# One encoder layer on one core: transposes and attention steps emitted at other places, row steps of two gate blocks reordered, finer splits, x loaded earlier

## The chip, the cores and the metric

The kernel runs on 1 core of one Trainium2 chip. The metric is the device time of one execution in microseconds. Before the change the median of 3 runs is 2099.92 us (2099.83 to 2100.81).

## What is computed

One layer of a bidirectional encoder for 256 tokens of width 2048, all in float32: a half-step SwiGLU feed-forward network (inner width 5632), a mixer of two attentions side by side, and a second half-step SwiGLU. Norms stand ahead of and behind each part.

```
def swiglu(h, w_gate, w_up, w_down):
    return (jax.nn.silu(h @ w_gate) * (h @ w_up)) @ w_down

f = swiglu(rmsnorm(x, ffn1_pre_g), ffn1_w_gate, ffn1_w_up, ffn1_w_down)
x = x + 0.5 * rmsnorm(f, ffn1_post_g)
h = rmsnorm(x, mix_pre_g)
qa, ka, va, qb, kb, vb, ga, gb = jnp.split(h @ w_in, SPLITS, axis=-1)
ga, gb = sigmoid(ga + bias_a), sigmoid(gb + bias_b)
out_a = windowed_gqa_sink(rope(qa), rope(ka), va, sink)              # 8 query heads, 2 key heads
out_b = differential_attention(rope(qb), rope(kb), vb, lam, subln_g) # 4 heads, two softmaxes each
x = x + rmsnorm((ga * (out_a @ w_proj_a) + gb * (out_b @ w_proj_b)) @ w_out, mix_post_g)
f = swiglu(rmsnorm(x, ffn2_pre_g), ffn2_w_gate, ffn2_w_up, ffn2_w_down)
x = x + 0.5 * rmsnorm(f, ffn2_post_g)
```

## The kernel before

The 256 tokens are two halves h0 and h1 of 128. A matrix product in float32 is three TensorE passes on parts rounded to a shorter format, hi and lo (`mm3`, `mm3s`: hi by hi, lo by hi, hi by lo; L257 to L259 in wide blocks, L200 to L202 elsewhere). All 400 MB of weights come from HBM in **units** of 1 MB (`load_unit`, on SP's queue). `emit_upto` splits each unit: ACT copies it to the short format (hi, the cast at L177), DVE subtracts to get lo (L179). A unit is one 128x2048 instruction on each, or four of 128x512 for unit 0 (L183). Two units are split ahead of the one in use.

A **tall** block makes 512 columns for both halves (`run_block`). A **wide** block makes 1024 columns for both halves in four banks (`run_wide`); its units are row steps of 256 rows, and each is N (24 matmuls, plain) or S (a Strassen step: seven products instead of eight, on sums of the weights that DVE makes at L188 to L190 and on sums of the inputs from `make_forms`, L394 to L402). `SKIND = "NSNSNSNN"` gives the kinds of the eight row steps of a gate or up block. Behind the last S step the extra products are folded into the banks: ACT copies one bank (L292), DVE adds the rest (L293 to L305). Only then do the banks come free for the block behind.

The blocks run in this order: ffn1; kb0, kb1, qb, vb, kv; ga0, qa, gb0, ga2 (gates and queries); the two branch projections and wo; ffn2. In each FFN column block 0 is tall; the first wide gate block, c == 1, is the one where the inputs' sums are made beside the matmuls.

What isn't on the main path is put between the matmuls. `later(fn, n)` defers a function by n calls of `pump()`, which each row step makes once. The rotary result of a query or key block (L641 to L648 on DVE) is transposed by TensorE in such a deferred function (`split_T`, L407, with the copies L408 on ACT and L409 on DVE), and so are the products of gate and up. The attentions are `pipeline`s of items: `ItemB` (8 items, stages s0 to s3 at L709 to L750) beside kv and ga0, `ItemA` (8 items, three stages, L766 to L807) beside gb0 and ga2; each `pump()` issues one step of the pipeline. `drain()` pumps until nothing is left, with no matmul between; it stands ahead of each pipeline and behind ga2. A gate block ends in four DVE instructions at L836 and four sigmoids on ACT at L839.

The order on each engine is not the order of the code: a scheduler of the compiler, with its own idea of the durations, places every instruction by its release and its priority. `tc.high_priority(HP)` lifts what it encloses. Each engine then runs its instructions strictly in that order and waits where one isn't ready.

Of the kernel before, what the change touches and what calls it, by code (L numbers as in the profile page):

```python
# [35 lines left out]
SKIND = "NSNSNSNN"  # L36
HP = 300
# [6 lines left out]
def encoder_layer(  # L44
# [89 lines left out]
    def add_wide(w, r0, rows, c0, kinds=None):  # L134
        kinds = kinds or "N" * (rows // 256)
        return add_units(w, r0, rows, c0, kinds), kinds

    loaded, emitted = {}, {}
    spill, paced = set(), set()
    lo_of, hi_of = {}, {}  # L140
# [25 lines left out]
    def emit_upto(i):  # L166
        for k in range(len(emitted), min(i + 1, len(units))):
# [58 lines left out]
    def run_block(start, nu, lhs, after, lag=0, pre=None, tail=None):  # L226

        acc = [acc_tile(), acc_tile()]
        for i in range(nu + lag):
# [12 lines left out]
            for h, u in ((0, i), (1, i - lag)):  # L242
# [8 lines left out]
                if u == nu - 1:  # L251
                    after(h, 0, acc[h])
# [8 lines left out]
    def run_wide(block, lhs, forms, after):  # L261


        start, kinds = block
        last_s = kinds.rfind("S")
        bank, opened = {}, set()
        end = len(kinds) - 1
# [8 lines left out]
        for u, kind in enumerate(kinds):  # L276
            w = weights(start + u)
            if kind == "S":
# [6 lines left out]
                order = ("P1", "P2", "P6", "Q5", "P3", "P7", "Q4") if u == last_s else                     ("P1", "P2", "P3", "Q5", "P7", "P6", "Q4")  # L285
                for o in order:
                    f = open_(o)
                    mm3s(bank[o], *ops[o], f, u == last_s, True)
                if u == last_s:
# [16 lines left out]
            else:  # L306
                order = (("P2", 0, 0), ("P3", 0, 1), ("X", 1, 1), ("Q4", 1, 0)) if last_s >= 0 else                     (("P2", 0, 0), ("P3", 0, 1), ("Q4", 1, 0), ("X", 1, 1))
                for o, h, c in order:
                    t = lhs(u, h)
                    for j in range(2):  # L310
                        f = open_(o)
                        closes = u == end or u == last_s - 1 and o == "X"
                        mm3s(bank[o], (t[:, 0, j, :], t[:, 1, j, :]), w, 2 * j + c, f, closes and j == 1, last_s >= 0)
                    if u == end:
# [154 lines left out]
    def ffn(post_g, pre, plan, lag, final, tail, x_src):  # L469
# [5 lines left out]
        def gate_up(c0, run_gate, run_up):  # L475
# [6 lines left out]
            def up_after(h, c, acc):  # L482
# [7 lines left out]
                later(tr, 2 if c0 + 1 in last_c or c0 == 0 else len(SKIND) - 1)  # L490
# [39 lines left out]
    def plan_ffn(w_gate, w_up, w_down):  # L530
        pl = {"gate": {}, "up": {}, "down": {}}
        for part, (c_lo, c_hi) in enumerate(PARTS):
            for c in range(c_lo, c_hi):
# [3 lines left out]
                elif c % 2:  # L537
                    pl["gate"][c] = add_wide(w_gate[0], 0, D, c * NC, SKIND)
# [28 lines left out]
    for b in (pm["kb", 0], plan2["gate"][0]):  # L567
        spill.add(b)
        paced.add(b + 3)

# [8 lines left out]
    load_unit(0, (2, 3))  # L579
    for h in range(2):  # L580
        load_x(h, 256, 1024)
    load_upto(1)
# [229 lines left out]
    def pipeline(items, offs):  # L812
        n = len(items)
        for t in range(n + offs[-1]):
# [10 lines left out]
    drain()  # L825
    ticker[0] = pipeline([ItemB(s, h, hh) for s in range(2) for h in range(2) for hh in range(2)], (0, 1, 2, 3))
# [38 lines left out]
    drain()  # L865
# [62 lines left out]
```

## Time and profile before

| what | value |
|---|---|
| median of 3 runs | 2099.92 us |
| the profiled execution | 2102.28 us |
| span of its trace, first to last instruction | 2100.5 us |
| TensorE (PE) busy | 2045.2 us, 97% |
| VectorE (DVE) busy | 1430.9 us, 68% |
| ScalarE (ACT) busy | 987.4 us, 47% |
| mean granted TensorE clock | 0.989 |
| DMA, mean over the span | 198 GB/s |

The page gives shares of the whole span. PE is nearly always busy, so what it loses lies in a few places, and those are found with the view of PE's waits and read in the timeline of the stretch: each row has the start, the length, the instruction, and in brackets the idle time before it and what ended it. A bracket of one engine names the instruction on another engine; that engine's timeline of the same stretch says why it came late.

### The profile page before, as it was taken

Reading aid. Unit: us, or ns where it says so; the run is one execution under the profiler, and the core shown is the slowest. Engines: PE = TensorE matmul, PEld = TensorE weight load, DVE = VectorE, ACT = ScalarE, POOL = GpSimd, SP = SyncE. Lnnn points to the kernel's source line nnn. Section 1 sums busy time; section 2 is a strip of 40 time slices with the busy share of each in tenths; the row PEclk is TensorE's granted clock in tenths of the full one; section 3 lists DMA queues with packets and bytes.
Section 4 is the critical chain, followed back from the end, with each engine's and each line's share of the span. In section 5 each row is a group of like instructions: output and inputs, shape, how many; then the busy total and the mean of one; then the engine's idle time right before and its main releaser. Section 6 shows DMA issues by size and latency. Waiting matters only on the chain. (4 is left out here: it accounts for less than half of the span.)

```text
span 2100.5 us, 22846 instructions
## 1 busy us (share of the span) xinstructions
PE 2045.2 (97%) x9193; PEld 1680.1 (80%) x9193; DVE 1430.9 (68%) x1400; ACT 987.4 (47%) x943; POOL 56.2 (3%) x91
## 2 busy tenths in 40 slices
PE   8999999999999989999899999999999999999997
PEld 6788887888877878888788888787888788887786
DVE  5884798647986575676664555577658885588854
ACT  6454455435553453455454344455454544454442
POOL 1000000000000010000000000000000000000000
PEclk9999999999999999999999999999999999999999
DMA  8546555676557646554445556554575565856662
GB/s 289 185 170 231 201 180 196 214 211 200 186 195 291 208 162 204 193 175 158 153 151 188 203 189 243 199 186 149 216 232 188 196 214 187 225 181 211 232 252 86
DMA packets 140571, 416.36 MB, mean 198 GB/s; under 512 B 8415, under 2 KB 9233, under 8 KB 139185
## 3 DMA queue, kind: packets, MB, share of 16 engines
q1 hardware_dynamic: 133872, 391.15, 54.0%
q0 software_dynamic: 6560, 23.75, 4.1%
q8 instruction: 72, 1.18, 0.2%
q14 instruction: 35, 0.28, 0.0%
q10 hardware_dynamic: 32, 0.01, 0.0%
HBM read 400.19 MB, written 14.68 MB: 198 GB/s over the span
## 5 line engine op out<-in xcount | busy, mean ns | idle before, releaser
L179 DVE TENSOR_TENSOR w<-raw,w 128x2048 fp32r<-128x2048 f32 (+2 forms) x365 | 796.5, 2184 | 500.3 <-ACT w L177 465.8
L177 ACT CAST w<-raw 128x2048 fp32r<-128x2048 f32 (+2 forms) x365 | 666.7, 1828 | 783.8 <-PE acc L258 605.4
L257 PE MATMUL acc<-w,xT 128*128 128x512 f32 x1368 | 536.6, 393 | 5.6 <-ACT t L292 4.0
L258 PE MATMUL acc<-w,xT 128*128 128x512 f32 x1368 | 534.1, 390 | 0.0
L259 PE MATMUL acc<-w,xT 128*128 128x512 f32 x1368 | 512.5, 391 | 0.6 <-DVE w L179 0.6
L257 PE MATMUL acc<-w,big 128*128 128x512 f32 x828 | 323.2, 391 | 3.3 <-ACT w L177 3.3
L258 PE MATMUL acc<-w,big 128*128 128x512 f32 x828 | 323.8, 391 | 0.0
L259 PE MATMUL acc<-w,big 128*128 128x512 f32 x828 | 317.6, 390 | 0.2 <-DVE w L179 0.2
L257 PEld LDWEIGHTS acc<-w,xT 128*128 128x128 f32 x1368 | 257.5, 188 | 61.9 <-ACT t L292 4.8
L259 PEld LDWEIGHTS acc<-w,xT 128*128 128x128 f32 x1368 | 257.5, 188 | 54.8 <-DVE w L179 1.4
L258 PEld LDWEIGHTS acc<-w,xT 128*128 128x128 f32 x1368 | 257.6, 188 | 52.0
L257 PEld LDWEIGHTS acc<-w,big 128*128 128x128 f32 x828 | 155.7, 188 | 36.4 <-ACT w L177 4.1
L259 PEld LDWEIGHTS acc<-w,big 128*128 128x128 f32 x828 | 155.6, 188 | 32.5 <-DVE w L179 0.6
L258 PEld LDWEIGHTS acc<-w,big 128*128 128x128 f32 x828 | 155.7, 188 | 31.9
L177 ACT CAST big<-raw 128x2048 fp32r<-128x2048 f32 x62 | 118.6, 1913 | 93.1 <-DVE raw L190 89.1
L179 DVE TENSOR_TENSOR big<-raw,big 128x2048 fp32r<-128x2048 f32 x62 | 141.2, 2286 | 20.7 <-ACT big L177 15.8
L201 PE MATMUL acc<-w,xT 128*128 128x512 f32 x208 | 83.0, 401 | 3.0 <-DVE xT L358 3.0
L200 PE MATMUL acc<-w,xT 128*128 128x512 f32 x208 | 82.0, 399 | 0.0
L202 PE MATMUL acc<-w,xT 128*128 128x512 f32 x208 | 80.4, 393 | 0.0
L257 PE MATMUL acc<-big,big 128*128 128x512 f32 x180 | 72.3, 402 | 6.1 <-ACT big L177 6.1
L200 PE MATMUL acc<-w,big 128*128 128x512 f32 x192 | 74.7, 389 | 0.0
L201 PE MATMUL acc<-w,big 128*128 128x512 f32 x192 | 74.7, 389 | 0.0
(186 smaller groups left out, 1744.7 us busy)
## 6 DMA issues: line engine op xcount, KB each, us to landing
raw<-in_ffn_w_down SPq DMA_DIRECT2D x88, 1024.0 KB, 5.2
raw<-in_w_in SPq DMA_DIRECT2D x68, 1024.0 KB, 5.0
raw<-in_ffn_w_up SPq DMA_DIRECT2D x58, 1024.0 KB, 5.1
raw<-in_ffn_w_gate SPq DMA_DIRECT2D x57, 1024.0 KB, 5.1
raw<-in_ffn_w_gate SPq DMA_DIRECT2D x60, 512.0 KB, 4.7
raw<-in_ffn_w_up SPq DMA_DIRECT2D x60, 512.0 KB, 4.7
raw<-in_w_out SPq DMA_DIRECT2D x16, 1024.0 KB, 5.0
f_dram<-t POOLq DMA_DIRECT2D x32, 256.0 KB, 5.8
```

The costliest lines, as they stand in the source:

```text
L177: nc.scalar.copy(hi[:, sl], raw[:, sl])
L179: nc.vector.tensor_tensor(lo[:, sl], raw[:, sl], f32(hi[:, sl]), ALU.subtract)
L200: nc.tensor.matmul(o, lhi, rhi, start=first, stop=False)
L201: nc.tensor.matmul(o, llo, rhi, start=False, stop=False)
L202: nc.tensor.matmul(o, lhi, rlo, start=False, stop=last)
L257: nc.tensor.matmul(o, t[0], w[0][:, q, :], start=first, stop=False, skip_group_check=skip)
L258: nc.tensor.matmul(o, t[1], w[0][:, q, :], start=False, stop=False, skip_group_check=skip)
L259: nc.tensor.matmul(o, t[0], w[1][:, q, :], start=False, stop=last, skip_group_check=skip)
```

## The change

The order of the row steps of the first wide gate block (c == 1) in both FFNs goes through a table, `FIRST`: N N S N S N S N instead of N S N S N S N N, with the same weights to the same inputs. Some units are split in two pieces of 1024 columns (`fine`): units 1 to 3, and five units each around the start of kb0 and of ffn2; unit 0 stays in four. `after` of a tall block is issued at high priority. The transposes of gate times up are deferred by 8 pumps instead of 7. At the start the columns 256 to 1024 of x are loaded ahead of the second half of unit 0, and the columns 1024 to 2048 ahead of unit 1. Both drains ahead of the attention pipelines and the one behind ga2 are gone: the pipelines wait 1 and 3 pumps first, in which the deferred transposes are issued beside matmuls. Lines of the changed kernel stand 1 to 5 further on (L407 becomes L409, L736 L740, L836 L841).

```diff
+FIRST = (0, 2, 1, 4, 3, 6, 5, 7)
...
-    def add_units(w, r0, rows, c0, kinds):
+    def add_units(w, r0, rows, c0, kinds, order=None):
 
         start = len(units)
-        r = r0
-        for k in kinds:
-            n, c = (512, NC) if k == "T" else (256, 2 * NC)
-            units.append((k, w[r:r + n, c0:c0 + c]))
-            r += n
-        assert r == r0 + rows
+        for i in order or range(len(kinds)):
+            n, c = (512, NC) if kinds[i] == "T" else (256, 2 * NC)
+            units.append((kinds[i], w[r0 + i * n:r0 + (i + 1) * n, c0:c0 + c]))
...
-                for j in [slice(i, i + 1) for i in range(4)] if k == 0 else [slice(0, 4)]:
+                for j in [slice(i, i + fine.get(k, 4)) for i in range(0, 4, fine.get(k, 4))]:
                     split(hi, lo, j)
...
                 if u == nu - 1:
-                    after(h, 0, acc[h])
+                    with tc.high_priority(HP):
+                        after(h, 0, acc[h])
...
-        for u, kind in enumerate(kinds):
-            w = weights(start + u)
+        for n, (u, kind) in enumerate(steps):
+            w = weights(start + n)
...
-                later(tr, 2 if c0 + 1 in last_c or c0 == 0 else len(SKIND) - 1)
+                later(tr, 2 if c0 + 1 in last_c or c0 == 0 else len(SKIND))
...
-                    pl["gate"][c] = add_wide(w_gate[0], 0, D, c * NC, SKIND)
+                    pl["gate"][c] = add_wide(w_gate[0], 0, D, c * NC, SKIND, FIRST if c == 1 else None)
...
+        fine.update({b + i: 2 for i in range(-1, 4)})
+
+    fine.update({0: 1, 1: 2, 2: 2, 3: 2})
...
     load_x(1, 0, 256)
-    load_unit(0, (2, 3))
     for h in range(2):
         load_x(h, 256, 1024)
-    load_upto(1)
+    load_unit(0, (2, 3))
     for h in range(2):
         load_x(h, 1024, 2048)
     load_upto(2)
...
-    def pipeline(items, offs):
+    def pipeline(items, offs, wait):
         n = len(items)
+        for _ in range(wait):
+            yield
...
-    drain()
-    ticker[0] = pipeline([ItemB(s, h, hh) for s in range(2) for h in range(2) for hh in range(2)], (0, 1, 2, 3))
+    ticker[0] = pipeline([ItemB(s, h, hh) for s in range(2) for h in range(2) for hh in range(2)], (0, 1, 2, 3), 1)
...
-    drain()
-    ticker[0] = pipeline([ItemA(h, p) for h in range(2) for p in range(4)], (0, 1, 2))
+    assert ticker[0] is None
+    ticker[0] = pipeline([ItemA(h, p) for h in range(2) for p in range(4)], (0, 1, 2), 3)
     gate_block("gb", D, 0)
     ga0, gb0 = gates.pop("ga"), gates.pop("gb")
     gate_block("ga", 0, 2)
-    drain()
+    assert ticker[0] is None
```

The diff doesn't tell where the instructions stand on their engines. First place, PE in the first wide gate block of ffn1, from the closing of the last Strassen bank to the first matmul of the up block (the first into `acc_917` before, into `acc_923` now); `big_` weights are the sums. Before:

```order
L259 MATMUL acc_676<-w_735,xT_295 128x512
L259 MATMUL acc_619<-w_735,xT_295 128x512
L259 MATMUL acc_626<-w_735,big_603 128x512
L257 MATMUL acc_917<-w_837,xT_134 128x512
L258 MATMUL acc_917<-w_837,xT_134 128x512
L257 MATMUL acc_694<-big_741,big_603 128x512
```

Now:

```order
L261 MATMUL acc_712<-w_771,xT_301 128x512
L261 MATMUL acc_625<-w_771,xT_301 128x512
L261 MATMUL acc_632<-w_771,big_601 128x512
L259 MATMUL acc_722<-big_708,big_582 128x512
L260 MATMUL acc_722<-big_708,big_582 128x512
L259 MATMUL acc_726<-big_708,big_582 128x512
L260 MATMUL acc_726<-big_708,big_582 128x512
L259 MATMUL acc_730<-big_708,big_582 128x512
L260 MATMUL acc_730<-big_708,big_582 128x512
L259 MATMUL acc_646<-big_708,xT_235 128x512
L260 MATMUL acc_646<-big_708,xT_235 128x512
L259 MATMUL acc_923<-w_834,xT_134 128x512
```

Before, two matmuls stand between the bank's last one (`acc_676`) and the up block's first; now ten stand there behind the last into `acc_712`. In all, PE's rows change only at the start, in these two blocks of each FFN, at the last matmuls ahead of kb0 and of ffn2, and from ga0 to ga2.

Second place, DVE at the end of ga0, where the last item of the B attention ends; `t_1083` before and `t_1086` now are its result (L736, L740), which PE transposes right ahead of qa; L325 and L327 make the norm's factor for it, and `w_` is the split of a unit. Before:

```order
L836 SCALAR_TENSOR_TENSOR t_1095_6841<-acc_6361,pnr_5259,t_991_6351 128x512
L836 SCALAR_TENSOR_TENSOR t_1097_6851<-acc_6368,pnr_5259,t_992_6353 128x512
L325 TENSOR_SCALAR bv_6780<-bss_6778 128x1
L836 SCALAR_TENSOR_TENSOR t_1098_6860<-acc_6375,pnr_5345,t_991_6351 128x512
L750 SCALAR_TENSOR_TENSOR big_6674<-tp_6785,gT,big_6674 128x128
L836 SCALAR_TENSOR_TENSOR t_1099_6869<-acc_6382,pnr_5345,t_992_6353 128x512
L736 TENSOR_SCALAR t_1083_6777<-at_6770,br_6782 128x256
L179 TENSOR_TENSOR w_6875<-raw_6872,w_6874 128x2048
```

Now:

```order
L841 SCALAR_TENSOR_TENSOR t_1094_6850<-acc_6328,pnr_5275,t_976_6318 128x512
L841 SCALAR_TENSOR_TENSOR t_1096_6860<-acc_6335,pnr_5275,t_977_6320 128x512
L841 SCALAR_TENSOR_TENSOR t_1097_6869<-acc_6342,pnr_5361,t_976_6318 128x512
L841 SCALAR_TENSOR_TENSOR t_1098_6878<-acc_6349,pnr_5361,t_977_6320 128x512
L180 TENSOR_TENSOR w_6891<-raw_6888,w_6890 128x2048
L327 TENSOR_SCALAR bv_6826<-bss_6824 128x1
L754 SCALAR_TENSOR_TENSOR big_6720<-tp_6831,gT,big_6720 128x128
L740 TENSOR_SCALAR t_1086_6823<-at_6816,br_6828 128x256
```

The result stood behind the fourth L836 and ahead of the unit's split; now its factor and it stand behind both the four L841 and the split.

Third place, PE from qa (bank `acc_1106`, short `acc_6899` and `acc_6915`) to gb0; `tp` is a transposed rotary result. Before:

```order
L259 MATMUL acc_6899<-w_7029,xT_5248 128x512
L407 MATMUL tp_7141<-ident,t_1128_7098 128x128 x4
L407 MATMUL tp_7149<-ident,t_1130_7110 128x128 x4
L407 MATMUL tp_7156<-ident,t_1132_7122 128x128 x4
L407 MATMUL tp_7163<-ident,t_1134_7134 128x128 x4
L257 MATMUL acc_7180<-w_7058,xT_5043 128x512
```

Now:

```order
L261 MATMUL acc_7187<-w_7075,xT_5055 128x512
L259 MATMUL acc_7166<-w_7104,xT_5082 128x512
L409 MATMUL tp_7195<-ident,t_1128_7114 128x128 x4
L260 MATMUL acc_7166<-w_7104,xT_5082 128x512
L261 MATMUL acc_7166<-w_7105,xT_5082 128x512
L259 MATMUL acc_7166<-w_7104,xT_5082 128x512
```

Before, the four transposes stood between the two blocks. Now the first stands behind 25 matmuls of gb0 (the rows above begin with the 24th), the second 12 further on, the third and the fourth together another 11 behind it.

## Rows read from the trace of the kernel before

**Rows 1.** Section 1 of the page: busy us, share of the span, instructions.
```profile
span 2100.5 us, 22846 instructions
...
PE 2045.2 (97%) x9193; PEld 1680.1 (80%) x9193; DVE 1430.9 (68%) x1400; ACT 987.4 (47%) x943; POOL 56.2 (3%) x91
```

**Rows 2.** Waits of PE: line waited for, us in total, times, longest.
```profile
PE tp L407 <- DVE t L648: 6.5, 3, 2.8
PE acc L257 <- ACT big L177: 6.1, 6, 1.5
```

**Rows 3.** Timeline of PE at the start: start us, us, instruction, [idle before <-releaser].
```profile
10.40 0.69 PE L350 MATMUL tp<-ident,big 128*128 128x128 f32 x2 [3.77 <-DMA big<-in_x]
...
11.72 0.78 PE L200 MATMUL acc<-w,xT 128*128 128x512 f32 x1
```

**Rows 4.** Timeline of ACT at the start.
```profile
14.05 1.91 ACT L177 CAST w<-raw 128x2048 fp32r<-128x2048 f32 x1 [1.32 <-DMA raw<-in_ffn_w_gate]
```

**Rows 5.** DMA view, 0 to 24 us: GB/s in 40 equal slices.
```profile
GB/s 0 0 5 189 177 360 331 352 312 111 52 195 335 399 410 422 405 410 396 393 403 389 430 416 382 396 389 386 393 389 382 382 389 386 386 389 386 393 386 382
```

**Rows 6.** Line L179 by form: xcount, duration ns min/median/max, forms.
```profile
L179 DVE TENSOR_TENSOR w<-raw,w x365: 691/2291/2294, 4.9 to 2076.3; 128x2048 fp32r<-128x2048 f32 x121, 128x1536 fp32r<-128x1536 f32 x60, 128x512 fp32r<-128x512 f32 x2
```

**Rows 7.** Timeline of PE, first wide gate block of ffn1.
```profile
91.87 0.50 PE L257 MATMUL acc<-w,xT 128*128 128x512 f32 x1 [2.19 <-ACT t L292]
...
93.75 0.79 PE L257 MATMUL acc<-big,big 128*128 128x512 f32 x1 [1.14 <-ACT big L177]
94.34 0.63 PE L258 MATMUL acc<-big,big 128*128 128x512 f32 x1
...
96.87 0.39 PE L258 MATMUL acc<-big,xT 128*128 128x512 f32 x1
```

**Rows 8.** Windows: us, busy (x) of PE, PEld, DVE, ACT, POOL, granted PE clock, DMA share, GB/s.
```profile
55.00:97.00 42.00, 38.37 (x164) 30.53 (x163) 39.50 (x47) 24.65 (x20) 0.00 (x0) 0.96 0.54 185
...
1012.00:1029.00 17.00, 10.52 (x45) 8.24 (x44) 14.53 (x22) 5.44 (x6) 0.00 (x0) 0.80 0.59 208
```

**Rows 9.** Timeline of PE, first wide gate block of ffn2.
```profile
1437.72 0.50 PE L257 MATMUL acc<-w,xT 128*128 128x512 f32 x1 [1.79 <-ACT t L292]
...
1440.00 0.79 PE L257 MATMUL acc<-big,big 128*128 128x512 f32 x1 [1.48 <-ACT big L177]
```

**Rows 10.** Timeline of PE, end of ffn1 to kb0.
```profile
746.18 1.11 PE L350 MATMUL tp<-ident,big 128*128 128x128 f32 x4 [3.73 <-DVE big L421]
```

**Rows 11.** Timeline of PE, end of ga0.
```profile
972.90 0.44 PE L746 MATMUL tp<-ident,t 128*128 128x128 f32 x2 [1.48 <-DVE t L736]
...
973.41 0.40 PE L258 MATMUL acc<-w,xT 128*128 128x512 f32 x1
973.64 0.40 PE L259 MATMUL acc<-w,xT 128*128 128x512 f32 x1
```

**Rows 12.** Timeline of DVE, end of ga0.
```profile
964.90 0.15 DVE L325 TENSOR_SCALAR bv<-bss 128x1 f32<-128x1 f32 x1 [0.45 <-ACT t L734]
...
965.78 0.48 DVE L736 TENSOR_SCALAR t<-at,br 128x256 f32<-128x256 f32 x1 [0.27 <-POOL br L327]
...
969.42 1.40 DVE L836 SCALAR_TENSOR_TENSOR t<-acc,pnr,t 128x512 f32<-128x512 f32 x2
...
970.80 0.74 DVE L836 SCALAR_TENSOR_TENSOR t<-acc,pnr,t 128x512 f32<-128x512 f32 x1
...
974.21 2.29 DVE L179 TENSOR_TENSOR w<-raw,w 128x2048 fp32r<-128x2048 f32 x1 [1.37 <-ACT w L177]
```

**Rows 13.** Timeline of PE, end of qa.
```profile
1018.01 0.66 PE L407 MATMUL tp<-ident,t 128*128 128x128 f32 x4 [1.10 <-DVE t L648]
1021.46 0.82 PE L407 MATMUL tp<-ident,t 128*128 128x128 f32 x4 [2.80 <-DVE t L648]
1024.86 1.97 PE L407 MATMUL tp<-ident,t 128*128 128x128 f32 x8 [2.58 <-DVE t L648]
```

**Rows 14.** Timeline of DVE, end of qa.
```profile
1024.13 1.29 DVE L648 TENSOR_TENSOR t<-t,t 128x512 f32<-128x512 f32 x2
```

More of the change, by code (lines that the diff above doesn't have):

```diff
@@ L118, in encoder_layer @@
     units = []
-    def add_units(w, r0, rows, c0, kinds):
+    def add_units(w, r0, rows, c0, kinds, order=None):
         start = len(units)
-        r = r0
-        for k in kinds:
-            n, c = (512, NC) if k == "T" else (256, 2 * NC)
-            units.append((k, w[r:r + n, c0:c0 + c]))
-            r += n
-        assert r == r0 + rows
+        for i in order or range(len(kinds)):
+            n, c = (512, NC) if kinds[i] == "T" else (256, 2 * NC)
+            units.append((kinds[i], w[r0 + i * n:r0 + (i + 1) * n, c0:c0 + c]))
+        assert n * len(kinds) == rows
         return start
@@ L132, in add_tall, with add_wide @@
         return add_units(w, r0, rows, c0, "T" * (rows // 512))
-    def add_wide(w, r0, rows, c0, kinds=None):
+    def add_wide(w, r0, rows, c0, kinds=None, order=None):
         kinds = kinds or "N" * (rows // 256)
-        return add_units(w, r0, rows, c0, kinds), kinds
+        order = order or range(len(kinds))
+        return add_units(w, r0, rows, c0, kinds, order), [(u, kinds[u]) for u in order]
     loaded, emitted = {}, {}
     spill, paced = set(), set()
+    fine = {}
     lo_of, hi_of = {}, {}
@@ L261, in run_wide @@
     def run_wide(block, lhs, forms, after):
-        start, kinds = block
-        last_s = kinds.rfind("S")
+        start, steps = block
+        last_s = max([n for n, (_, k) in enumerate(steps) if k == "S"], default=-1)
         bank, opened = {}, set()
-        end = len(kinds) - 1
+        end = len(steps) - 1
         def open_(o):
@@ L284, in run_wide @@
                        "Q5": (s1, w[2:4], 1), "P7": (s3, w[2:4], 3), "P6": (s2, w[2:4], 2), "Q4": (a22, w[2:4], 0)}
-                order = ("P1", "P2", "P6", "Q5", "P3", "P7", "Q4") if u == last_s else                     ("P1", "P2", "P3", "Q5", "P7", "P6", "Q4")
+                order = ("P1", "P2", "P6", "Q5", "P3", "P7", "Q4") if n == last_s else                     ("P1", "P2", "P3", "Q5", "P7", "P6", "Q4")
                 for o in order:
                     f = open_(o)
-                    mm3s(bank[o], *ops[o], f, u == last_s, True)
-                if u == last_s:
+                    mm3s(bank[o], *ops[o], f, n == last_s, True)
+                if n == last_s:
                     with tc.high_priority(HP):
@@ L311, in run_wide @@
                         f = open_(o)
-                        closes = u == end or u == last_s - 1 and o == "X"
+                        closes = n == end or n == last_s - 1 and o == "X"
                         mm3s(bank[o], (t[:, 0, j, :], t[:, 1, j, :]), w, 2 * j + c, f, closes and j == 1, last_s >= 0)
-                    if u == end:
+                    if n == end:
                         with tc.high_priority(HP):
```

## The prediction

> **What bounds the kernel now.** I read the page's busy shares first: TensorE (PE) works 2045.2 of 2100.5 us [rows 1], so the kernel is bound by PE, and only what PE loses can be won. The profiled execution took 2102.28 us, 1.78 more than its span, and lies 2.36 above the median of the runs; all terms below are differences, so I take their sum off the median. The view of PE's waits then says for whom it waits: the largest entry is the transposes of rotary results behind DVE's L648 (6.5 us in three waits), then wide blocks behind ACT's cast of the summed weights (6.1 in six) [rows 2]. The timelines of these places come last. Two prices recur in them. Undisturbed, matmuls of 512 columns follow each other by 0.23 us [rows 11]. Behind some waits they follow by 0.42 to 0.59 for a while: from 94.34 to 96.87 stand six of them [rows 7]; that is the lower of the clock's two levels, 1.2 instead of 2.4 GHz. Behind the wait of 1.48 us at the end of ga0 the spacing is 0.23 at once [rows 11], so a short wait alone isn't followed by it. The stretch of the lower clock at 93.75 costs 3.12 us for seven matmuls that otherwise take 1.6, so 1.5 us [rows 7].
>
> **The change part by part.**
>
> *Start.* PE's transposes wait 3.77 us for x's columns from 256 on and the first matmul starts at 11.72 [rows 3]. The second half of unit 0, 512 KB, was queued ahead of them on SP and is now behind; the DMA engines move 390 to 420 KB a us here [rows 5], so x lands 1.3 us sooner and the first matmul starts near 10.4: -1.3. Against it, the last 1 MB of x now stands ahead of unit 1, which lands 2.6 us later than the 14.05 at which its cast began [rows 4]. The matmuls of unit 0 and the transposes for them run to about that time plus the cast, so I count nothing; the halves of the finer split let the first matmuls begin after half a cast. If the later unit shows in full it costs 2.6, so the term runs from -1.3 to +1.3, and -1.8 if the lower clock ends sooner as well. I take -1.3.
>
> *Finer splits.* A DVE subtraction of 512 columns takes 0.69 us, one of 2048 takes 2.29 [rows 6]. On the line between them 1024 columns take 1.22, two pieces 2.45: 0.16 more for each of the 13 units that are split, 2.1 in all. Beside it the first half is ready 1.1 us sooner. At the places where it is done DVE waits for ACT, or PE for x, so I count 0 and keep up to +2.1. The Trainium skill, page "VectorE: DVE Perf Modes", section "The TRN2 errata — SBUF-src ops pay a fixed extra latency per instruction", speaks against this part: every instruction exposes a fixed latency of SBUF, a large tile once and many small ones each time. By that rule the pieces cost and bring nothing, which is the +2.1 end; the two durations agree with a fixed part, and whether it is covered they don't tell.
>
> *First wide gate block of each FFN.* In ffn1 PE waits 2.19 us at 91.87 for the ACT copy that empties the extra Strassen bank, then 1.14 at 93.75 for the cast of the sums, and runs at the lower clock until 96.87 [rows 7]. In the 42 us of this block PE is busy 38.37 and DVE 39.50 [rows 8]: DVE is nearly full, because the inputs' sums, three S units and the folding of banks come together. The idle 3.6 and the 1.5 of the clock make 5.1. Now the first S step comes third, the sums of the inputs have 24 more matmuls to be made in, and ten matmuls instead of two stand between the bank's last product and the first matmul that needs it empty: 2.3 us, against a cast ahead of the copy (1.91 [rows 4]) and the copy of a quarter as many columns (0.5 by that row), 2.4 together from the matmul before. DVE's work doesn't grow; if its row of splits up to the last sum's lo part ends as before, by the window's end at 97, it is in time: PE asks for that part only 47 matmuls (10.7 us) behind the point where it began to wait, 89.7, so near 100.4. So I take -5.1, with 3 us kept as the poor end (a part of the wait comes back behind the folding) and -6 as the good one. ffn2 has the same block with waits of 1.79 and 1.48 [rows 9] and the same stretch behind: -5.1 again, ends -3 and -6.5.
>
> *Ahead of kb0 and ffn2.* PE waits 3.73 us for the first normalized columns of x at 746.18 [rows 10]. h0 now closes four matmuls earlier against h1 (0.9 us), and its addition on DVE goes ahead of a split; half a split (1.2) still stands ahead of the power's input. I take -0.6, from 0 to -1.6. At ffn2 the ACT scaling, behind a whole cast, keeps its place: 0.
>
> *End of the B attention.* The drain ahead of it cost PE nothing visible, but the pipeline starts one pump later and so ends one later, at the very end of ga0. The transposes of its last result stand right ahead of qa on PE; all of qa is queued behind them. Before, they waited 1.48 us [rows 11]. DVE now runs the four gate additions (1.40 for two, 0.74 the single one [rows 12]: 2.8), then a whole split (2.29), and only then the factor and the result; from the factor's first step to the result lie 0.9 at an earlier item (964.90 to 965.78 [rows 12]). That is 6.0 us behind the last product, which PE fills with 0.2 of transposes: a wait of 5.8, 4.3 more than before. It is longer than the 3.73 of [rows 10], so I add one stretch of lower clock, 1.4: +5.7. The ends are 0 (the old wait stays) and +6.5.
>
> *End of qa.* The drain put four sets of transposes between qa and gb0. PE waits 1.10, 2.80 and 2.58 us before them [rows 13], 6.5 together, and the mean clock of these 17 us is 0.80 [rows 8]: 6.8 us at the lower level, of which the waits can hold up to 5.4, so between 0.7 and 2.1 of work is lost as well; I take 1.9, since the eight transposes of 1024.86 take 1.97, more than twice the 0.66 of the first four [rows 13]. Now the first set stands behind 25 matmuls of gb0 (5.7 us), the second 12 further on, the others 11 behind. qa ended near 1016.8 (the start of the first wait), so they fall at 1022.5, 1025.5 and 1028.4. DVE had the first two results when PE's waits ended, at 1018.0 and 1021.5, and the last two at 1025.4 [rows 13, 14], with copies of transposed sets in between that now come later. Nothing is late: -8.4, ends -6.5 and -8.6. The transposes themselves stay, as do their copies. The A pipeline starts three pumps later: one more of its items meets the end of gb0, where the order of additions, exponentials and table loads on DVE and ACT is that which the item before it has now; I count 0.
>
> *Sum.* -1.3 - 5.1 - 5.1 - 0.6 + 5.7 - 8.4 = -14.8: 2099.92 - 14.8 = **2085.1 us** (the profiled execution 2087.5).
>
> **The rivals.**
> 1. *The wait in the wide gate blocks only moves.* DVE's 39.50 of 42 us [rows 8] speaks for it: the folding now meets the first splits of the up block. Each block then gives 2.5 instead of 5.1: 2090.3.
> 2. *The result of the last B item isn't late*, because ACT's cast for the unit comes sooner than I think and the old wait stays: 2085.1 - 5.7 = 2079.4. Against it speaks that the split stands ahead of it in any case.
> 3. *Slower.* The stages of a B item now stand in a row on PE, with no matmul between scores, weights and values, where one to three stood. If each of the 8 items waits for DVE or ACT, PE pays 8 times; from 1.9 us an item (8 x 1.9 = 15) the whole gain is gone. With 2.3 and a stretch of lower clock (1.4) each it is 29.6: 2114.7. Against it: each stage uses a result issued a pump earlier, some 24 matmuls or 5.5 us.
> 4. *The start doesn't do what it says*, because PE waits for unit 1 instead: +1.3 for -1.3, 2087.7.
> 5. *The pieces cost what they add*, the rule named above: +2.1, 2087.2.
>
> **How the numbers follow.** The forecast has 0.55, rival 1 0.2, rival 2 0.1, rival 3 0.05, rivals 4 and 5 together 0.1. The forecast's own spread (a us at each place) is about 2081 to 2089, which holds rivals 4 and 5 too. The range goes over rivals 1 and 2 and some way on, where two of the poor ends meet (3 us of each gate block and +6.5 at the end of ga0: 2090.1; with a qa of -6.5 2092.0): 2077.5 to 2093. A measurement of this kernel can tell about 0.2%, 4.2 us, from no change. Faster than that needs a gain over 4.2: all but rival 3 and a heap of poor ends, 0.91; within it 0.05; slower 0.04.
>
> **What would show it.** In the profile after, the transposes of rotary results are gone from PE's waits, and gb0 starts behind qa without a gap. The two gate blocks show no wait for the ACT copy over 0.5 us and no 0.42 spacing. The first matmul starts near 10.4. At the end of ga0 the largest new entry stands, transposes of L750 behind DVE's L740, near 5.8 us. The forecast is wrong if waits stand beside the B items, if DVE's folding makes PE wait in the up block, or if the wait at ga0's end is short.

## The result and the profile after

The changed kernel takes **2080.20 us** (median of 4 runs, 2079.09 to 2080.92) against 2100.36 us before (2099.83 to 2100.99), measured beside it: a ratio of 0.9903 with a 95% interval from 0.9886 to 0.9921, 20.2 us less. The forecast was 2085.1, in a range of 2077.5 to 2093: the sign and the range hold, the gain was put 5.4 us too low. The profiled execution took 2079.09 us.

The page's first section, which answers to [rows 1], shows PE 8.7 us less busy with the same 9193 matmuls. The number of matmuls is the same, so they took less time: the mean granted clock rose from 0.989 to 0.994.

```profile
span 2077.3 us, 22878 instructions
...
PE 2036.5 (98%) x9193; PEld 1675.9 (81%) x9193; DVE 1431.5 (69%) x1413; ACT 987.9 (48%) x956; POOL 55.9 (3%) x91
```

The view of PE's waits (us in total, times, longest) answers to [rows 2]. The rotary transposes behind DVE (6.5 us) are gone, and so are two of the six waits for ACT's cast of the sums. The transposes of the last B item, 1.5 us before ([rows 11] has the wait), now lead with 5.6. The wait for ACT's scaling at the start of ffn2 (last line) was 1.4 before; PE's rows lose nothing there all the same (table below).

```profile
PE tp L750 <- DVE t L740: 5.6, 1, 5.6
PE acc L259 <- ACT big L178: 3.5, 4, 0.9
...
PE acc L201 <- ACT xT L358: 2.3, 1, 2.3
```

Now the places. PE at the start, against [rows 3]:

```profile
8.78 0.69 PE L352 MATMUL tp<-ident,big 128*128 128x128 f32 x2 [0.97 <-DMA big<-in_x]
...
10.12 0.78 PE L201 MATMUL acc<-w,xT 128*128 128x512 f32 x1
```

PE in the first wide gate block of ffn1, against [rows 7]: the first matmul of the up block (90.53) follows after 0.04 us of idle time, and behind it matmuls soon come every 0.23 us (the last row holds three).

```profile
90.10 0.39 PE L260 MATMUL acc<-big,xT 128*128 128x512 f32 x1
90.53 0.50 PE L259 MATMUL acc<-w,xT 128*128 128x512 f32 x1
90.86 0.40 PE L260 MATMUL acc<-w,xT 128*128 128x512 f32 x1
91.10 0.85 PE L261 MATMUL acc<-big,big 128*128 128x512 f32 x3
```

The view of windows for the block's 42 us, against [rows 8]: PE busy for all of it, at the full clock, and DVE at 40.38 us fuller than before.

```profile
55.00:97.00 42.00, 41.96 (x188) 34.22 (x187) 40.38 (x46) 23.48 (x18) 0.00 (x0) 1.00 0.54 183
```

PE at kb0, against [rows 10]:

```profile
734.79 0.83 PE L352 MATMUL tp<-ident,big 128*128 128x128 f32 x4 [2.64 <-DVE big L423]
...
736.92 0.63 PE L203 MATMUL acc<-big,xT 128*128 128x512 f32 x1
```

DVE ahead of kb0, first before and then now: the addition of h0 (L443, now L445) stood behind the whole split of a unit; now it stands ahead of that split's two halves, and one half stands ahead of the power's input (L461).

```profile
739.22 2.29 DVE L179 TENSOR_TENSOR w<-raw,w 128x2048 fp32r<-128x2048 f32 x1 [0.84 <-ACT w L177]
741.43 0.68 DVE L443 TENSOR_TENSOR big<-acc,big 128x512 f32<-128x512 f32 x1
```
```profile
729.02 0.69 DVE L445 TENSOR_TENSOR big<-acc,big 128x512 f32<-128x512 f32 x1 [1.73 <-PE acc L203]
...
730.36 1.22 DVE L180 TENSOR_TENSOR w<-raw,w 128x1024 fp32r<-128x1024 f32 x1
731.50 0.15 DVE L461 SCALAR_TENSOR_TENSOR qv<-q,fss 128x1 f32<-128x1 f32 x1
```

PE and then DVE at the end of ga0, against [rows 11, 12]. On DVE the four gate additions (2.72 us) and the split (2.28) stand ahead of the factor at 963.27 and of the result at 964.14. Behind PE's wait matmuls follow by 0.43 us.

```profile
964.68 0.69 PE L750 MATMUL tp<-ident,t 128*128 128x128 f32 x2 [5.62 <-DVE t L740]
...
965.59 0.63 PE L260 MATMUL acc<-w,xT 128*128 128x512 f32 x1
966.02 0.63 PE L261 MATMUL acc<-w,xT 128*128 128x512 f32 x1
```
```profile
958.43 2.72 DVE L841 SCALAR_TENSOR_TENSOR t<-acc,pnr,t 128x512 f32<-128x512 f32 x4
961.07 2.28 DVE L180 TENSOR_TENSOR w<-raw,w 128x2048 fp32r<-128x2048 f32 x1
963.27 0.14 DVE L327 TENSOR_SCALAR bv<-bss 128x1 f32<-128x1 f32 x1
...
964.14 0.48 DVE L740 TENSOR_SCALAR t<-at,br 128x256 f32<-128x256 f32 x1 [0.47 <-POOL br L329]
```

PE behind qa, against [rows 13]: the sixteen transposes (the last eight stand in one row) have no idle time ahead of them.

```profile
1015.84 0.60 PE L409 MATMUL tp<-ident,t 128*128 128x128 f32 x4
...
1019.04 0.60 PE L409 MATMUL tp<-ident,t 128*128 128x128 f32 x4
...
1022.00 1.03 PE L409 MATMUL tp<-ident,t 128*128 128x128 f32 x8
```

Because both kernels issue 9193 matmuls, the time from one ordinal to another can be compared place by place. I did this for the two profiles shown so far and for a second profile of each kernel (the runs before again and after again, below). Us, after minus before:

| place | forecast | first profiles | second profiles |
|---|---|---|---|
| start | -1.3 | -1.8 | +0.1 |
| first wide gate block, ffn1 | -5.1 | -5.8 | -7.2 |
| first wide down block, ffn1 | 0 | -2.5 | -0.1 |
| start of kb0 | -0.6 | -1.8 | -1.9 |
| end of the B attention | +5.7 | +5.5 | +5.9 |
| end of qa and gb0 | -8.4 | -9.0 | -9.2 |
| start of ffn2 | 0 | 0 | 0 |
| first wide gate block, ffn2 | -5.1 | -6.8 | -6.8 |
| first wide down block, ffn2 | 0 | -0.8 | +1.0 |
| whole span | -14.8 | -23.2 | -18.2 |

The medians, 20.2 us apart, lie between the two columns. The -1.9 of kb0 in the last column is -3.6 behind the wait and +1.7 some 25 us later; the second profile of the changed kernel, below, shows why. The start is set by when x lands, and one pair of profiles doesn't tell it from chance: in ten profiles with the loads and splits of the changed kernel PE begins its 151st instruction between 39.35 and 41.52 us, 40.27 in the mean, and in the two of before at 41.15 and 40.45.

### The profile page after: what moved, and what is told of

Same layout as the page of the kernel before. It is cut to its first block, busy times and chain, and to the rows that moved or that the text cites. A ratio compares the mean times of both kernels' runs of the same rounds, so it can differ in the third digit from the quotient of the medians.

```text
span 2077.3 us, 22878 instructions
## 1 busy us (share of the span) xinstructions
PE 2036.5 (98%) x9193; PEld 1675.9 (81%) x9193; DVE 1431.5 (69%) x1413; ACT 987.9 (48%) x956; POOL 55.9 (3%) x91
## 5 line engine op out<-in xcount | busy, mean ns | idle before, releaser
L180 DVE TENSOR_TENSOR w<-raw,w 128x2048 fp32r<-128x2048 f32 (+3 forms) x376 | 796.5, 2123 | 492.5 <-ACT w L178 458.7
L178 ACT CAST w<-raw 128x2048 fp32r<-128x2048 f32 (+3 forms) x376 | 667.6, 1782 | 782.7 <-PE acc L260 607.7
L259 PE MATMUL acc<-w,big 128*128 128x512 f32 x828 | 322.8, 390 | 1.1 <-ACT w L178 1.1
L260 PE MATMUL acc<-w,big 128*128 128x512 f32 x828 | 323.4, 391 | 0.0
L261 PE MATMUL acc<-w,big 128*128 128x512 f32 x828 | 318.0, 390 | 0.4 <-DVE w L180 0.4
L178 ACT CAST big<-raw 128x2048 fp32r<-128x2048 f32 (+1 forms) x64 | 118.9, 1860 | 89.2 <-DVE raw L191 85.4
L180 DVE TENSOR_TENSOR big<-raw,big 128x2048 fp32r<-128x2048 f32 (+1 forms) x64 | 141.5, 2219 | 23.0 <-ACT big L178 18.0
L201 PE MATMUL acc<-w,big 128*128 128x512 f32 x192 | 74.7, 389 | 0.0
L202 PE MATMUL acc<-w,big 128*128 128x512 f32 x192 | 74.7, 389 | 0.0
L203 PE MATMUL acc<-w,big 128*128 128x512 f32 x192 | 74.0, 389 | 0.0
```

The lines of the kernel that those rows point to most:

```text
L178: nc.scalar.copy(hi[:, sl], raw[:, sl])
L180: nc.vector.tensor_tensor(lo[:, sl], raw[:, sl], f32(hi[:, sl]), ALU.subtract)
L201: nc.tensor.matmul(o, lhi, rhi, start=first, stop=False)
L202: nc.tensor.matmul(o, llo, rhi, start=False, stop=False)
L203: nc.tensor.matmul(o, lhi, rlo, start=False, stop=last)
L259: nc.tensor.matmul(o, t[0], w[0][:, q, :], start=first, stop=False, skip_group_check=skip)
```

## The experiments

All but the two second profiles of an unchanged kernel are edits of the changed kernel. They were run in three groups; the medians of the kernel before beside them were 2099.17, 2098.89 and 2099.62 us, where it was 2100.36 beside the changed kernel. PE's rows of the changed kernel came again in two of the groups, at 2080.69 (the transposes deferred by 7) and 2081.94 us (one run), against 2080.20. So differences of medians under some 2 us aren't settled by the times; PE's rows at the place say more. The high priority of `after`, the drain ahead of the B attention and the one behind ga2 were not undone by themselves.

### Parts of the change undone

**The gate blocks' row steps in the old order.**

```diff
-                    pl["gate"][c] = add_wide(w_gate[0], 0, D, c * NC, SKIND, FIRST if c == 1 else None)
+                    pl["gate"][c] = add_wide(w_gate[0], 0, D, c * NC, SKIND, None)
```

> The changed kernel, but with the row steps of both first wide gate blocks again in the order N S N S N S N N. Theory: in these blocks DVE has more to do than fits beside the matmuls when the first Strassen step comes second, and the row order alone is the cure; the waits of PE for the ACT copy (about 2.2 and 1.8 us) and for the cast of the sums (1.1 and 1.5 us) with the stretch of low clock come back, 5.6 us in ffn1 and 6.6 in ffn2, so 2080.2 + 12.2 = 2092.4 us. Rival: the earlier start or the finer splits gave DVE the lead it lacked; then at most half comes back, up to 2086 us.

Measured 2095.16 us (2091.04 to 2097.26, eight runs), ratio 0.9977 (0.9966 to 0.9987). The part is worth 15 us by the medians, more than any theory gave, and the rival, by which at most half comes back, is out. These runs scatter over 6 us where the others scatter over 1 to 3. The profiled execution was the fastest, 2091.04. Its waits are back. In its timeline of PE, first in ffn1 and then in ffn2, the same two waits are followed by something different. In ffn1 thirteen matmuls follow by 0.43 us (92.92 to 98.04), in ffn2 none: 0.23 at once.

```profile
90.05 0.50 PE L259 MATMUL acc<-w,xT 128*128 128x512 f32 x1 [1.79 <-ACT t L294]
...
92.32 0.80 PE L259 MATMUL acc<-big,big 128*128 128x512 f32 x1 [1.54 <-ACT big L178]
92.92 0.63 PE L260 MATMUL acc<-big,big 128*128 128x512 f32 x1
...
98.04 0.50 PE L260 MATMUL acc<-w,xT 128*128 128x512 f32 x1
```
```profile
1429.36 0.50 PE L259 MATMUL acc<-w,xT 128*128 128x512 f32 x1 [1.79 <-ACT t L294]
...
1431.64 0.50 PE L259 MATMUL acc<-big,big 128*128 128x512 f32 x1 [1.54 <-ACT big L178]
1431.97 0.39 PE L260 MATMUL acc<-big,big 128*128 128x512 f32 x1
1432.21 0.39 PE L259 MATMUL acc<-big,big 128*128 128x512 f32 x1
```

So the two waits, 3.3 us a block, are the fixed price, and the lower clock adds up to 2.7 us: the fourteen matmuls from 92.32 on take 6.1 us, those from 1431.64 on 3.3. I took a second profile of this kernel, and one of the kernel before, to see whether that length belongs to the place.

> The kernel of e1_first_off once more (first wide gate block in its old order). In e1 the two waits came back alike in both FFNs (1.79 and 1.54 us), but 13 matmuls at 0.43 us stood behind them in ffn1 and none in ffn2, while in the profile of before 6 and 11 stood there. Theory: the waits are fixed by the order (1.8 and 1.5 again, within 0.1), and how long the lower clock lasts behind them differs from execution to execution; so the counts differ from 13 and 0, and the time is 0.23 us a matmul off e1's 2091.0, up to 2097. Rival: the place sets it, and 13 and 0 come again.

2090.91 us: the waits again (1.91 and 1.43 in ffn1, 1.80 and 1.54 in ffn2), and again twelve slow matmuls in ffn1 and none in ffn2. For this kernel the rival stands: the place looks fixed in both profiles. But both are executions of 2091 us with a mean granted clock of 0.993; the five above 2094 us had 0.989 to 0.991. A clock lower by 0.002 to 0.004 over 2090 us is 4 to 8 us by estimate, and their excess is 4 to 6. That would fit a lower clock that lasts longer in those, but run by run the mean clock doesn't tell the time (the slowest has 0.991), and no profile shows a place; the cause of their excess stays open.

> The kernel before, a second profile. Theory: the waits of the first down blocks for ACT's cast (1.94 us in ffn1, 1.31 in ffn2, 3.3 together) follow the landing of a transfer and differ between executions, as in the nine profiles of the changed kernel and its variants (1.0 to 2.3 together): here under 3. Rival: the change itself took 2 us there, and 3.3 comes again within 0.3. The two waits of each gate block stay (2.19 and 1.14; 1.79 and 1.48), the count of slow matmuls behind them moves off 6 and 11.

2100.22 us. Here the length does change at one place: six matmuls at 0.43 us in ffn1 in the first profile (94.34 to 96.87, [rows 7]), thirteen now (93.62 to 98.74), behind waits of the same sum, 3.33 and 3.34 us.

```profile
90.76 0.50 PE L257 MATMUL acc<-w,xT 128*128 128x512 f32 x1 [1.80 <-ACT t L292]
...
93.03 0.79 PE L257 MATMUL acc<-big,big 128*128 128x512 f32 x1 [1.54 <-ACT big L177]
93.62 0.63 PE L258 MATMUL acc<-big,big 128*128 128x512 f32 x1
...
98.74 0.57 PE L258 MATMUL acc<-w,xT 128*128 128x512 f32 x1
```

And the waits of the first down blocks, 3.3 us in the first profile of before, are 1.0 in this one (view of PE's waits):

```profile
PE acc L257 <- ACT w L177: 1.0, 2, 0.5
```

The profiles of the changed kernel and its variants have 1.0 to 2.3 there. So the -2.5 and -0.8 of the first column aren't the change's doing: the first profile of before had a bad draw. Four loads of 1 MB each are issued on POOL's queue from 630.21 to 638.82 us in that profile, while the unit that PE waits for is under way (its cast begins at 640.55); whether they make it late I didn't try.

**The drain ahead of the A attention put back.**

```diff
-    assert ticker[0] is None
-    ticker[0] = pipeline([ItemA(h, p) for h in range(2) for p in range(4)], (0, 1, 2), 3)
+    drain()
+    ticker[0] = pipeline([ItemA(h, p) for h in range(2) for p in range(4)], (0, 1, 2), 0)
```

> The changed kernel with the drain ahead of the A attention again and no pumps waited there. Theory: the four sets of transposes between qa and gb0 wait for DVE's rotary results again, 1.1 + 2.8 + 2.6 us, with the low clock behind: 9.0 us, 2089.2 us. Rival: the late start of the A pipeline costs something at the end of gb0 that comes back here, so that only about 4 us are lost: 2084 us.

2090.33 us (2089.61 to 2091.84), ratio 0.9959 (0.9944 to 0.9974): 10.1 above the changed kernel, a little over the theory's 9; the rival's 4 is out. The waits of before are back in PE's timeline, 6.2 us together, and the slow transposes with them:

```profile
1012.12 0.66 PE L409 MATMUL tp<-ident,t 128*128 128x128 f32 x4 [1.09 <-DVE t L652]
1015.58 1.12 PE L409 MATMUL tp<-ident,t 128*128 128x128 f32 x4 [2.79 <-DVE t L652]
1018.98 1.97 PE L409 MATMUL tp<-ident,t 128*128 128x128 f32 x8 [2.29 <-DVE t L652]
```

From there to the middle of gb0 PE's rows lose 9.5 us against the changed kernel's. So the transposes are late when nothing stands between qa's last product and them.

**The loads at the start in the old order.**

```diff
+    load_unit(0, (2, 3))
     for h in range(2):
         load_x(h, 256, 1024)
-    load_unit(0, (2, 3))
+    load_upto(1)
```

> The changed kernel with the loads at the start in the old order (second half of unit 0 ahead of x's columns from 256 on, unit 1 ahead of those from 1024 on). Theory: the first matmul comes 1.6 us later and nothing is won back: 2080.2 + 1.8 = 2082.0 us. Rival: unit 1 arriving sooner makes up for it within the first tall block: 2080.2 us, PE level with the changed kernel by 45 us.

2081.85 us (2081.53 to 2083.09), ratio 0.9920 (0.9906 to 0.9935): 1.65 lost, and 1.2 against the kernel with 7 pumps in the same group. The theory's 1.8 fits, but the times don't tell it from the rival, by which nothing is lost. In the profiles the x columns land anywhere within 1.6 us for one and the same order of loads; the last but one transposes of the start began at 8.78 in the changed kernel, at 9.07 in its second profile, and, in a variant with the same loads (the one with later transposes, below), at 10.42:

```profile
10.42 0.69 PE L352 MATMUL tp<-ident,big 128*128 128x128 f32 x2 [3.64 <-DMA big<-in_x]
```

With the old order they began at 10.22 here, and at 10.40 [rows 3] and 10.03 in the kernel before. The new order brings x sooner on the whole, but one profile can't price it.

**Units 1 to 3 split whole, x still first.**

```diff
-    fine.update({0: 1, 1: 2, 2: 2, 3: 2})
+    fine.update({0: 1})
```

> The changed kernel with units 1 to 3 split whole again, x still loaded first. Theory: PE asks for unit 1's rounded part at 18.98 us and for its lo part at 20.15, where the half pieces are ready at 18.8 and 20.05; whole pieces are ready some 1 and 1.2 us later, so PE waits 1 to 2 us: 2081.2 to 2082.2 against 2080.2. Rival (the pieces cost their fixed part and bring nothing): 3 x 0.06 less on DVE, 2080.0 or a little under.

2083.46 us (2083.00 to 2084.26), ratio 0.9924 (0.9907 to 0.9940). One run of the changed kernel in the same group took 2081.94, so 1.5 to 3.3 us are lost. PE now waits for unit 1, whose two halves it met in time: 0.53 us at 20.25 for ACT's part, and then for DVE's:

```profile
22.57 0.50 PE L203 MATMUL acc<-w,xT 128*128 128x512 f32 x1 [1.13 <-DVE w L180]
```

Its 151st instruction on PE begins at 41.78 us, later than in any of the ten profiles with the splits, and later than in the kernel before.

**The splits around kb0 and ffn2 taken out.**

```diff
-        fine.update({b + i: 2 for i in range(-1, 4)})
```

> The changed kernel without the splits in two pieces around the starts of kb0 and of ffn2 (unit 0 to 3 as changed). Theory: the pieces let h0 close four matmuls sooner and its addition pass a split on DVE; without them PE waits 3.7 us instead of 2.6 ahead of kb0 and the place costs 1.75 us more, at ffn2 nothing changes: 2082.0 us. Rival, by the Trainium skill's page VectorE: DVE Perf Modes, section The TRN2 errata: the pieces only cost their fixed part, so without them it is faster, by up to 1.6 us: 2078.6 us.

2082.10 us (2080.36 to 2083.21), ratio 0.9920 (0.9906 to 0.9935): 1.9 lost by the medians and 1.4 against the kernel with 7 pumps in the same group, whose runs overlap with these, so the times alone don't settle it. The profile does: kb0's wait is back at before's length, and PE loses 1.5 us there and nothing at ffn2's start, as the theory has it. First PE, then DVE:

```profile
736.99 1.12 PE L352 MATMUL tp<-ident,big 128*128 128x128 f32 x4 [3.73 <-DVE big L423]
```
```profile
730.03 2.29 DVE L180 TENSOR_TENSOR w<-raw,w 128x2048 fp32r<-128x2048 f32 x1 [0.84 <-ACT w L178]
732.24 0.68 DVE L445 TENSOR_TENSOR big<-acc,big 128x512 f32<-128x512 f32 x1
```

The high priority of `after` is still in this kernel, yet PE's last matmuls ahead of kb0 and of ffn2 stand in the order of before again, and h0's addition stands behind the whole split. So the priority alone doesn't bring the new order; the pieces do. Whether they need the priority as well, no run shows.

**The transposes of gate times up deferred by 7 pumps, as before.**

```diff
-                later(tr, 2 if c0 + 1 in last_c or c0 == 0 else len(SKIND))
+                later(tr, 2 if c0 + 1 in last_c or c0 == 0 else len(SKIND) - 1)
```

> The changed kernel with the transposes of gate times up deferred by 7 pumps again. Theory: no instruction stands elsewhere, so the time is that of the changed kernel, 2080.2 us within 1 us, and every wait that depends on order alone is the same to 0.1 us; what differs between the two profiles (the waits at the first down block of ffn1 near 632 us and of ffn2 near 1965 us above all) is set by how the loads of several queues mix, not by the change. Rival: those two waits are part of the change's gain and come out as in the changed kernel, 0.5 and 0.6 us.

2080.69 us (2079.89 to 2081.42), ratio 0.9913 (0.9896 to 0.9929). The scheduler gives PE the same rows, so this is a control: half a microsecond is what the medians of two equal orders differ by here.

**The changed kernel again.**

> The changed kernel, a second profile. Theory: the rows of PE and the waits behind other engines come again within 0.1 us (5.6 us for the result of the last B item, 2.64 at kb0, 2.26 at ffn2's start), no wait and no slow matmul in the gate blocks; what differs is x's landing (first matmul between 10.1 and 11.9 us) and the first down blocks (1.0 to 2.3 us together): span 2077 to 2080. Rival: waits at the gate blocks or at gb0 appear in some executions.

2081.94 us. The waits of 5.6, 3.5, 2.6 and 2.3 us come again to a tenth. What differs is x's first columns, the waits for DVE's part of the transposed inputs (3.4 us where 3.0 stood) and the down blocks (1.9 together where 1.1 stood); no wait and no slow matmul stands in the gate blocks. One thing nobody forecast differs as well. Behind the 2.64 us at kb0 the first profile has seven slow matmuls (a row of 0.63 us is shown above), this one none; here the slow ones stand behind another wait 25 us later, 2.07 us, which is in both profiles, and in the first is followed by the full clock.

```profile
735.87 0.83 PE L352 MATMUL tp<-ident,big 128*128 128x128 f32 x4 [2.64 <-DVE big L423]
...
737.97 0.40 PE L201 MATMUL acc<-big,xT 128*128 128x512 f32 x1
...
761.06 0.50 PE L202 MATMUL acc<-w,xT 128*128 128x512 f32 x1 [2.07 <-DVE xT L360]
...
764.53 0.63 PE L202 MATMUL acc<-w,xT 128*128 128x512 f32 x1
```

### The new wait at the end of ga0

**The B pipeline starts at once.**

```diff
-    ticker[0] = pipeline([ItemB(s, h, hh) for s in range(2) for h in range(2) for hh in range(2)], (0, 1, 2, 3), 1)
+    ticker[0] = pipeline([ItemB(s, h, hh) for s in range(2) for h in range(2) for hh in range(2)], (0, 1, 2, 3), 0)
```

> The changed kernel, but the B attention's pipeline starts without the extra pump (still without the drain). Theory: the extra pump alone made the last item's result late at the end of ga0; its transposes wait 1.5 us instead of 5.6 and no stretch of low clock follows: 5.4 us faster than the changed kernel, 2074.8 us. Rival: the removed drain made it late; then the wait of 5.6 us stays, 2080.2 us.

2075.29 us (2074.51 to 2076.24), ratio 0.9887 (0.9872 to 0.9901): 4.9 below the changed kernel. The wait shrinks to before's 1.48, and no slow matmul follows it. PE waits for no other item, though the drain of before isn't there either, so the rival is out: the pump of waiting bought nothing, it only pushed the last item to where DVE was busy.

```profile
963.74 0.44 PE L750 MATMUL tp<-ident,t 128*128 128x128 f32 x2 [1.48 <-DVE t L740]
963.93 0.48 PE L259 MATMUL acc<-w,xT 128*128 128x512 f32 x1
```

**The result's transposes one pump later.** The pipeline waits as in the changed kernel; only the last stage moves.

```diff
-    ticker[0] = pipeline([ItemB(s, h, hh) for s in range(2) for h in range(2) for hh in range(2)], (0, 1, 2, 3), 1)
+    ticker[0] = pipeline([ItemB(s, h, hh) for s in range(2) for h in range(2) for hh in range(2)], (0, 1, 2, 4), 1)
```

> The changed kernel with the extra pump, but the last stage of each B item (its transposes) comes one pump later still, so that the last one stands beside qa's first row steps. Theory: the late result costs only because PE's queue has its transposes ahead of all of qa; with matmuls ahead of them neither the wait nor the low clock is left, 7.2 us faster than the changed kernel: 2073.0 us. Rival: DVE's late work (gate additions, the split, the factor) holds qa in any case, through the banks or the split; then PE waits about as long for another instruction, 2079 to 2081 us.

2074.75 us (2074.09 to 2075.10), ratio 0.9883 (0.9866 to 0.9899): 5.5 below the changed kernel, and the wait is gone. On DVE the result still stands behind the four additions (959.50, 2.95 us) and the split, and is made at 965.44; PE doesn't wait for it.

```profile
962.37 2.28 DVE L180 TENSOR_TENSOR w<-raw,w 128x2048 fp32r<-128x2048 f32 x1
...
965.44 0.48 DVE L740 TENSOR_SCALAR t<-at,br 128x256 f32<-128x256 f32 x1 [0.21 <-POOL br L329]
```

At that place PE's rows gain 7.3 us against the changed kernel's, as expected, and the rival is out. The time missed the forecast by 1.8; in this profile x landed late, and the start lost 1.8, which is one execution and need not hold for the median.

**The same, with ACT's cast of the fourth unit behind the starts of kb0 and of ffn2 held back.** PE waits 2.26 us at ffn2's start for an ACT scaling that stands behind a cast; here the cast is queued behind the first scalings.

```diff
-                nc.scalar.copy(hi[:, sl], raw[:, sl])
+                with queued(hi_of.get(0) if k in paced else None):
+                    nc.scalar.copy(hi[:, sl], raw[:, sl])
...
+                hi_of.clear()
...
-    ticker[0] = pipeline([ItemB(s, h, hh) for s in range(2) for h in range(2) for hh in range(2)], (0, 1, 2, 3), 1)
+    ticker[0] = pipeline([ItemB(s, h, hh) for s in range(2) for h in range(2) for hh in range(2)], (0, 1, 2, 4), 1)
```

> As e4 (the last stage of the B items one pump later still), and ACT's cast of the fourth unit behind the starts of kb0 and of ffn2 is placed behind the first scalings of the transposes instead of ahead of them. Theory: at ffn2's start PE waits 2.3 us for these scalings, which stand behind that cast, and then runs at the low clock; with the cast behind them about 3.4 us are won beside the 7.2 of e4: 2069.6 us. Rival: the scalings are late for another reason (ACT's square ahead of them, DVE's sums), and the time is that of e4, 2073 us.

2072.49 us (2072.15 to 2073.45), ratio 0.9875 (0.9861 to 0.9890): the fastest of all, 7.7 below the changed kernel, but 2.9 above the theory. Most of the gain is the later transposes; against them alone (0.9883) the intervals overlap, and so what the held cast adds isn't settled by the times; against that kernel's, PE's rows gain 0.9 us at ffn2's start, where the theory had 3.4. There the wait for ACT falls to 0.60 us (PE's timeline, at 1332.25), but the next operand, DVE's, is 1.03 late (at 1333.78): the wait moved half way, and slow matmuls still follow.

## Why the prediction was right, and where it was off

**The first wide gate blocks** were the term most off in size: -5.1 each, measured -5.8 and -7.2 in ffn1 and -6.8 twice in ffn2. The 3.3 us of waits were read rightly and are gone, and the ten matmuls ahead of the bank's next use cover the copy but for 0.04 us. Two terms were mis-sized. The 1.5 us for the lower clock came from the one stretch of [rows 7], with six slow matmuls, and was carried over to ffn2; eleven stand there in both profiles of before, and thirteen in ffn1 in the second, which is 2.3 to 2.7 us. And a wait costs some 0.27 us more than its entry says: a matmul is shown with 0.39 us but the next follows after 0.23, so 0.16 of it counts as work ahead of a wait, and the first one behind it keeps the next back for 0.34, not 0.23. With 0.5 for two waits and 0.8 to 1.2 for the longer stretch, 5.1 becomes 6.4 to 6.8; with the short stretch of ffn1's first profile it becomes 5.6, where 5.8 was measured. Undoing the part cost 12 us in the two profiles and 15 by the medians; the 3 us between them have no place in any profile.

**The end of qa** was forecast at -8.4 and came to -9.0 and -9.2; putting the drain back cost 10.1. The waits were right; three of them at 0.2 to 0.3 more than their entries would make up the difference, which is argued here and not shown by a run. The transposes are met in time at each of the three places, as worked out.

**The end of the B attention** was right in place, cause and size: +5.7 forecast, +5.5 and +5.9 measured, a wait of 5.62 where 5.8 was expected, seven matmuls at the lower clock. Both experiments on it remove it by different means, so the cause is shown: DVE's additions and split stand between the product and its transposes. Rival 2, in which the cast comes sooner and the old wait stays, is out.

**The start of kb0** gave -1.8 and -1.9 for -0.6: right in mechanism, too small in size, and beyond the term's own end of -1.6. DVE's rows show what was forecast, h0's addition ahead of a split and half a split ahead of the power's input; with the pieces taken out both the order and the 3.73 us are back. The wait fell by 1.1, not 0.6, and the lower clock behind it, which the term left out, gave the rest: from the first transpose to PE's 25th instruction behind it, 7.73 us became 7.03 in the first pair. In the second pair 8.05 became 5.54, but 1.7 us of that came back behind the wait of 2.07 us, so the nearness of -1.8 and -1.9 is chance.

**The start** was forecast at -1.3, and the pairs of profiles have -1.8 and +0.1; by the means of the ten profiles and the two of before it is about -0.5 (40.27 against 40.80), so the term is right in sign at best, and a gain of 1.3 isn't shown. The later unit 1 was counted at nothing, since half pieces would let PE begin. They do, but that is worth 1.5 to 3.3 us, so the pieces aren't a term of 0 either: without them the earlier x is eaten up by the wait for unit 1 (rival 4, by another cause). The spread between the profiles goes with the landing of x.

**The pieces' cost** of up to +2.1, rival 5, didn't come. Two pieces of 1024 columns take 2.36 us, one of 2048 takes 2.29, so a pair costs 0.07 where 0.16 was assumed, 0.9 for all 13.

```profile
18.87 2.36 DVE L180 TENSOR_TENSOR w<-raw,w 128x1024 fp32r<-128x1024 f32 x2 [0.32 <-ACT w L178]
```

The Trainium skill, page "VectorE: DVE Perf Modes", section "The TRN2 errata — SBUF-src ops pay a fixed extra latency per instruction", tells of such a fixed cost, and the row agrees in kind. It didn't decide the sum: without the pieces PE waits longer at both places, 3.73 us for 2.64 ahead of kb0 (1.5 us in PE's rows) and 0.53 and 1.13 for unit 1 (1.5 to 3.3 us by the times).

**Rival 1** (the wait only moves into the up block) didn't come: DVE has 40.38 of 42 us to do and PE waits for nothing. **Rival 3** (each B item waits) didn't come either: with and without the pump of waiting, PE waits for no item but the last. The down blocks, which no term spoke of, show no part of the change; they make profiles of one kernel differ, by 2.3 us of wait in that of before.

So the 5.4 us that the forecast was short are, by the means of the two columns: 3.1 in the gate blocks, 1.3 at kb0 and 0.7 at qa. The start, put 0.4 too well, goes against them. That makes 4.7; the rest lies within what the start and the down blocks vary by.

## What to carry to other kernels

A wait that takes the place of a removed one is found by following the last item of a shifted pipeline to the engine that makes its result: it stood behind 5 us of other work in DVE's row, and moving only the consumer one step later gave back all that the change had lost there (7.3 us in PE's rows, where the change had lost 5.5). Price a wait of the tensor engine with the stretch of lower clock that follows, and take that from more than one stretch. Where a transfer sets a wait, take a second profile of the same kernel before giving the difference to a change.

## What was not expected of the hardware

- The lower clock behind the same waits isn't of one length. Behind waits of 1.8 and 1.5 us stood no slow matmuls (ffn2 of the changed kernel with the old order of row steps, twice) or twelve and thirteen (ffn1 of the same); at one place of the kernel before six in one execution and thirteen in another. What decides it these runs don't show.
- It needn't stand behind the same wait either. In the changed kernel the wait of 2.64 us at kb0 was followed by seven slow matmuls in one execution and by none in the other; there they stood behind a wait of 2.07 us, 25 us later.
- A single wait of 1.48 us was followed by the full clock in the kernel before and in the variant that starts the B pipeline at once. One of 2.26 us at ffn2's start had slow matmuls behind it in the changed kernel, and none in that variant; its rows gain 1.2 us there behind the same wait.
- x's columns, loaded in the same order, were ready to be transposed at 8.78 us in one execution of the changed kernel and at 9.07 in the other; in the variant with later transposes it was 10.42, with the same loads.
